# The order of TensorE's instructions in the attention: the scheduler's or the program's

## The chip, the cores and the metric

The kernel runs on one core of a Trainium2 chip. The core has a matrix engine (TensorE, PE in the rows; its weight loads are PEld), a vector engine (VectorE, DVE), an engine for activations (ScalarE, ACT), GpSimd (POOL) and SyncE (SP), which issues most of the loads. Each engine takes its own instructions from a queue of its own, and they wait for each other by semaphores. The metric is the time of one execution on the device in microseconds.

## The reference

One sequence of 512 tokens with 1024 features passes a state-space layer with a gated FFN, then an attention layer with a second gated FFN. The change is in the attention, which has 16 heads of 64 features:

```python
k, v = split(rms_norm(h, kv_norm) @ w_kv);  k = rms_norm(k per head);  q = rms_norm(xn @ w_q per head)
z = (q . k) / 8;  causal = k_pos < q_pos
log_beta = log_sigmoid(z);  log_1m = where(causal, log_beta - z, 0)
later = reverse cumsum of log_1m over the keys - log_1m
w = where(causal, exp(log_beta + later), 0)
out = w @ v;  h = h + out @ w_o
```

## The kernel before

The kernel is written with a layer that records instructions and orders them when the program is built: a scheduler goes through them with estimated durations and sets the order on each engine, by readiness and by their place in the program. A stretch of the program inside `tc.manual_schedule(engines={...})` keeps its written order on the engines named. The state-space layer's part has such a stretch for TensorE; the attention before has none.

The matrices are held as sums of two halves of lower precision (hi and lo), so a product with a weight matrix is three matmuls. Weights arrive by DMA (`t_wraw`); ScalarE makes `t_whi` (L116 or L119) and VectorE `t_wlo` (L130 or L133).

The attention's program is one list of TensorE work woven from two. The main list is the projection of k, q and v for four groups of four heads (L457 to L459, 12 matmuls at a step; `project`), and after it the output projection (L249 to L251, `wo_part`). The side list is the attention of eight pairs of heads. Group 0 is projected first; then `MAIN_RATIO` (0.792) side steps are taken for each main step, and `WO_RATIO` (0.743) in the output projection. A side step ends at each "|" of this list, which is gone through once for each pair p ("-" means pair p - 1, "+" pair p + 1):

```python
PAIR = (
    "|", "z Y0", "z X0", "|", "z X1", "p- A", "t- C0", "z Y1", "t- C1", "p- C", "|", "|", "|", "z Z", "tr+ 0",
    "tr+ 2", "t A0", "|", "tr+ 1", "t B", "|", "|", "p B", "|", "tr+ 3", "|", "t A1",
)
```

- "tr": L516, four transposes that turn the keys or queries of one head (0: keys of head 0, 1: queries of head 0, 2 and 3: of head 1) into PSUM bank 5 or 7. Queries are copied out by ScalarE (L520). Keys are copied out three times, one after the other: L524 (VectorE), L525 (ScalarE), L526 (VectorE).
- "z": L535, the scores of some blocks, into banks 2 to 4. ScalarE takes two sigmoids of them (L557, L558), VectorE a reversed running product by blocks (L564) and the product of both (L565), which is the weight `a_w`.
- "t": L579, four transposes of blocks of `a_w` into bank 5 or 7; ScalarE copies them out to `a_wt` (L581). Transposes of "tr" and "t" take banks 5 and 7 by turns.
- "p": L590, the value products of head 0 and head 1 into the lower and upper 64 partitions of bank 6. "p B" has two of 256 columns, "p A" two of 384 and two of 128, "p C" two of 512. After "p C" the bank is copied out (L608 or L164).

On VectorE and ScalarE there is also the work on the projections: L469 and L464 copy the projection's banks 0 and 1 out, L471 squares them, L474 sums, L475 to L207 are a chain of small operations for the norm, L483 applies it, L489 and L490 split the result into halves. L647 adds the output projection to the stream.

Of the kernel before, what the change touches and what calls it, by code (L numbers as in the profile page):

```python
# [17 lines left out]
DC = D // P  # L18
# [132 lines left out]
def split_x(e, srcs, gain, tag="x"):  # L151

    nc = e.nc
    hi = [e.tile([P, T], F32R, f"{tag}hi{i}") for i in range(len(srcs))]
    lo = [e.tile([P, T], F32R, f"{tag}lo{i}") for i in range(len(srcs))]
    for i, s in enumerate(srcs):
        split_one(e, s, hi[i], lo[i], None if gain is None else gain[:, i : i + 1])
    return hi, lo


def split_one(e, s, hi, lo, gain=None):
    nc = e.nc
    if gain is None:
        nc.scalar.copy(hi, s)  # L164
        nc.vector.tensor_tensor(out=lo, in0=s, in1=hi, op=ALU.subtract)
    else:
        nc.scalar.activation(hi, s, AF.Copy, scale=gain)
        nc.vector.scalar_tensor_tensor(out=lo, in0=s, scalar=gain, in1=hi, op0=ALU.mult, op1=ALU.subtract)  # L168
# [41 lines left out]
def sum_sq(e, pool, srcs, v=True):  # L210

    nc = e.nc
    acc = e.pt(pool, [P, T], F32, "ssacc")
    for i, s in enumerate(srcs):
        t = e.pt(pool, [P, T], F32, "sstmp", 2) if i else acc
        nc.scalar.activation(t, s, AF.Square)
        if i:
            (nc.vector if v else nc.gpsimd).tensor_tensor(out=acc, in0=acc, in1=t, op=ALU.add)
    return acc


def rstd_cols(e, acc, bank=None):

    nc = e.nc
    ps = e.bank(bank)
    for tb in range(4):
        nc.tensor.matmul(ps[:, tb : tb + 1], acc[:, tb * P : (tb + 1) * P], e.ones[:, 0:1], start=True, stop=True)  # L227
    ms = e.tile([P, 4], F32, "rsms")
    nc.vector.tensor_scalar(out=ms, in0=ps[:, 0:4], scalar1=1.0 / D, scalar2=EPS, op0=ALU.mult, op1=ALU.add)
    r = e.tile([P, 4], F32, "rstd4", 2)  # L230
    rsqrt(e, r, ms, [P, 4], "rs")
    return r
# [15 lines left out]
def mm3(nc, ps, whi, wlo, xhi, xlo, start, stop):  # L248
    nc.tensor.matmul(ps, whi, xhi, start=start, stop=False)  # L249
    nc.tensor.matmul(ps, whi, xlo, start=False, stop=False)  # L250
    nc.tensor.matmul(ps, wlo, xhi, start=False, stop=stop)  # L251
# [131 lines left out]
def attn_consts(e, pool):  # L383
    nc = e.nc
    c = {}
    c["identr"] = e.pt(pool, [P, P], F32R, "identr")
    nc.vector.tensor_copy(c["identr"], e.ident)

    c["edge"] = e.pt(pool, [P, T], F32, "edge")
    nc.gpsimd.memset(c["edge"], 0.0)  # L390
    nc.gpsimd.affine_select(
        out=c["edge"], in_=c["edge"], compare_op=ALU.not_equal, fill=1.0, base=T - P - 1, pattern=[[-1, T]],
        channel_multiplier=1)
    return c


MAIN_RATIO = 0.792
WO_RATIO = 0.743
# [9 lines left out]
WO_PARTS = ((0, 4), (4, 6), (6, 8))  # L408
# [231 lines left out]
def wo_part(e, ws, o, pairs, last):  # L640

    nc = e.nc
    hi = {}
    lo = {}

    def add(d, ps):
        nc.vector.tensor_tensor(out=e.hT[d], in0=ps, in1=e.hT[d], op=ALU.add)  # L647

    if not last:
        for i in pairs:  # L650
            if i >= DIRECT:
                hi[i], lo[i] = o[i]
                continue
            hi[i] = e.tile([P, T], F32R, f"xhi{i}")
            lo[i] = e.tile([P, T], F32R, f"xlo{i}")
            split_one(e, o[i], hi[i], lo[i])
        n = DC // len(pairs)
        for c in range(0, DC, n):
            whi, wlo = ws.take()
            for d in range(c, c + n):  # L660
                ps = e.bank(d % 2)
                col = slice((d - c) * P, (d - c + 1) * P)
                for j, i in enumerate(pairs):
                    mm3(nc, ps, whi[:, j, col], wlo[:, j, col], hi[i], lo[i], j == 0, j == len(pairs) - 1)
                    yield
                add(d, ps)
    else:
        w = {}
        for d0, d1 in ((0, LAST_BANKS), (LAST_BANKS, DC)):
            pss = [e.bank(d) for d in range(d0, d1)]  # L670
            for j, i in enumerate(pairs):
                if i not in w:
                    while i >= len(o):
                        yield
                    hi[i], lo[i] = o[i]
                    w[i] = ws.take()
                whi, wlo = w[i]
                for d, ps in zip(range(d0, d1), pss):
                    col = slice(d * P, (d + 1) * P)
                    mm3(nc, ps, whi[:, 0, col], wlo[:, 0, col], hi[i], lo[i], j == 0, j == len(pairs) - 1)  # L680
                    yield
                    if j == len(pairs) - 1:
                        add(d, ps)


def attention(e, ws, grow, r4=None):

    nc = e.nc
    with e.tc.tile_pool(name="attn", bufs=1, reuse_waits="tile") as pool:
        xhi, xlo = split_x(e, e.hT, None)  # L690
        if r4 is None:
            r4 = rstd_cols(e, sum_sq(e, pool, e.hT, False), 7)
        c = attn_consts(e, pool)
        a = Attention(e, pool, ws, c, grow, xhi, xlo, r4)
        for _ in a.project(0):
            pass
        side = a.schedule()
        n = main = 0
        for g in range(1, 4):
            for _ in a.project(g):  # L700
                main += 1
                while n < main * MAIN_RATIO:
                    next(side, None)
                    n += 1
        n = main = 0
        for lo, hi in WO_PARTS:
            last = hi == DC
            while len(a.o) < (lo + 1 if last else hi):
                next(side)
            for _ in wo_part(e, ws, a.o, range(lo, hi), last):  # L710
                main += 1
                while n < main * WO_RATIO:
                    next(side, None)
                    n += 1

G = 64
NP = 32
# [759 lines left out]
def trunk(tc, a, out):  # L1477
    with ExitStack() as ctx:
        e = Env(ctx, tc)
        nc = e.nc  # L1480
        w_up, w_down = a["ffn_w_up"], a["ffn_w_down"]
        v = Vectors(e, a)
        gkv, gb = v.va[:, 0:8], v.va[:, 8:16]
        ws = WStream(
            e,
            win_plan(a["a_w_in"][0]) + glu_plan(a["a_w_glu"][0]) + ffn_plan(w_up[0], w_down[0], False)
            + attn_plan(a["w_kv"], a["b_w_q"][0], gkv, gb) + wo_plan(a["b_w_o"][0]) + ffn_plan(w_up[1], w_down[1], True))
        s5(e, ws, a["a_norm"][0], a["x"][0], a["a_lam_re"][0], a["a_lam_im"][0], a["a_log_dt"][0], a["a_b_re"][0],
           a["a_b_im"][0], a["a_c_re"][0], a["a_c_im"][0], a["a_d"][0], v.load)
        r4 = ffn(e, ws, v.va[:, 16:24], v.cw[0], v.cb[0])  # L1490
        attention(e, ws, v.gr[0], r4)
        ffn(e, ws, v.va[:, 24:32], v.cw[1], v.cb[1], out[0])
# [21 lines left out]
```

## Time and profile before

| | us |
|---|---|
| median of 3 runs | 1261.51 (1259.55 to 1262.16) |
| the profiled execution | 1260.37 |
| its span | 1258.6 |
| TensorE busy | 1218.1 |
| VectorE busy | 780.2 |
| ScalarE busy | 542.2 |

The span is the time from the first to the last instruction of the profiled execution; the execution's own time has 1.8 us around it. An engine's busy time counts each moment once, also where several of its instructions overlap. The attention takes the time from 612 us to about 881 us, where the last value products are, and the end of the output projection after that; a stretch is given in microseconds from the span's start. In the timeline, an instruction's length reaches beyond the start of the next, since matmuls overlap; what an instruction costs the queue is the time from its start to the next one's start. A value product of 32-bit numbers shows as two instructions there.

### The profile page before, as it was taken

To read this page: it belongs to the slowest core of one execution; us is meant where nothing else is said; L and a number is where in the kernel's file an instruction comes from. 1 tells how busy PE (TensorE), PEld (TensorE's weight loads), DVE (VectorE), ACT (ScalarE), POOL (GpSimd) and SP (SyncE) were. 2 spreads that over 40 slices of the span, in tenths; PEclk is the share of its full clock that TensorE was granted. 3 is DMA by queue.
4 is the path that set the end of the run, shared out by engine and by line. 5 is a ranking of instruction groups with operands and counts; after the bars stand their busy time and mean duration, and the time that the engine had idled before them with its cause. 6 is when DMAs were issued, how large, how long until landed. Compare 5 with 4: busy or idle time off the path is not lost. (4 is left out here: it accounts for less than half of the span.)

```text
span 1258.6 us, 17176 instructions
## 1 busy us (share of the span) xinstructions
PE 1218.1 (97%) x6815; PEld 1013.4 (81%) x6815; DVE 780.2 (62%) x1252; ACT 542.2 (43%) x869; POOL 146.3 (12%) x133
## 2 busy tenths in 40 slices
PE   7687899999999999999999999999999999999998
PEld 7677687888888888888999888876788888888887
DVE  9888644867655564333579798875775555562222
ACT  7554543445333333222357675644553343332110
POOL 5869540000000000000000000000300000000000
PEclk9898999999999999999999999999999999999999
DMA  7333232333333333333232111111223333322330
GB/s 204 86 86 89 71 86 89 96 100 99 89 97 101 100 90 92 98 96 95 90 96 68 51 59 56 55 51 51 84 84 101 90 94 101 101 96 88 119 116 34
DMA packets 162379, 111.68 MB, mean 89 GB/s; under 512 B 7452, under 2 KB 151868, under 8 KB 162236
## 3 DMA queue, kind: packets, MB, share of 16 engines
q1 hardware_dynamic: 161724, 109.55, 29.6%
q8 instruction: 53, 0.87, 0.3%
q10 hardware_dynamic: 576, 1.05, 0.2%
q14 instruction: 26, 0.21, 0.1%
HBM read 101.93 MB, written 2.10 MB: 83 GB/s over the span
## 5 line engine op out<-in xcount | busy, mean ns | idle before, releaser
L249 PE MATMUL b<-t_xhi,t_whi 128*128 128x512 f32 x864 | 336.9, 392 | 1.4 <-ACT p_w L1322 1.4
L250 PE MATMUL b<-t_xlo,t_whi 128*128 128x512 f32 x864 | 337.1, 391 | 0.8 <-DVE t_xlo L168 0.7
L251 PE MATMUL b<-t_xhi,t_wlo 128*128 128x512 f32 x864 | 337.3, 391 | 0.2 <-DVE t_wlo L130 0.2
L116 ACT CAST t_whi<-t_wraw 128x1024 fp32r<-128x1024 f32 (+1 forms) x166 | 172.6, 1042 | 364.1 <-PE b L250 243.8
L130 DVE TENSOR_TENSOR t_wlo<-t_wraw,t_whi 128x1024 fp32r<-128x1024 f32 x152 | 184.9, 1218 | 155.3 <-ACT t_whi L116 154.3
L249 PEld LDWEIGHTS b<-t_xhi,t_whi 128*128 128x128 f32 x864 | 162.3, 188 | 37.6 <-issue 2.1
L250 PEld LDWEIGHTS b<-t_xlo,t_whi 128*128 128x128 f32 x864 | 162.4, 188 | 36.5 <-DVE t_xlo L168 2.7
L251 PEld LDWEIGHTS b<-t_xhi,t_wlo 128*128 128x128 f32 x864 | 162.4, 188 | 34.7 <-DVE t_wlo L130 0.6
L457 PE MATMUL b<-t_whi,t_xhi 128*128 128x256 f32 x384 | 109.6, 286 | 0.0
L458 PE MATMUL b<-t_wlo,t_xhi 128*128 128x256 f32 x384 | 109.2, 285 | 0.0
L459 PE MATMUL b<-t_whi,t_xlo 128*128 128x256 f32 x384 | 108.7, 285 | 0.0
L314 DVE TENSOR_TENSOR p_fg<-b,p_rsrow 128x512 f32<-128x512 f32 x44 | 30.4, 691 | 87.0 <-PE b L251 80.6
L457 PEld LDWEIGHTS b<-t_whi,t_xhi 128*128 128x128 f32 x384 | 73.3, 191 | 1.6 <-issue 1.2
L459 PEld LDWEIGHTS b<-t_whi,t_xlo 128*128 128x128 f32 x384 | 73.1, 191 | 1.5 <-issue 1.4
L458 PEld LDWEIGHTS b<-t_wlo,t_xhi 128*128 128x128 f32 x384 | 73.5, 191 | 0.3
L325 DVE TENSOR_TENSOR p_fv<-b,p_rsrow 128x512 f32<-128x512 f32 x44 | 30.4, 690 | 69.6 <-PE b L251 69.6
L249 PE MATMUL b<-p_ahi,t_whi 128*128 128x512 f32 x176 | 69.3, 394 | 0.0
L250 PE MATMUL b<-p_alo,t_whi 128*128 128x512 f32 x176 | 69.3, 394 | 0.0
L251 PE MATMUL b<-p_ahi,t_wlo 128*128 128x512 f32 x176 | 69.3, 394 | 0.0
L348 PE MATMUL b<-t_wlo,p_ahi 128*128 128x512 f32 x176 | 69.3, 394 | 0.0
L347 PE MATMUL b<-t_whi,p_ahi 128*128 128x512 f32 x176 | 69.0, 392 | 0.0
L349 PE MATMUL b<-t_whi,p_alo 128*128 128x512 f32 x176 | 68.3, 388 | 0.0
(305 smaller groups left out, 1917.3 us busy)
## 6 DMA issues: line engine op xcount, KB each, us to landing
t_wraw<-in_ffn_w_up_dram SPq DMA_DIRECT2D x88, 512.0 KB, 3.9
t_wraw<-in_ffn_w_down_dram SPq DMA_DIRECT2D x30, 512.0 KB, 3.4
t_wraw<-in_a_w_glu_dram SPq DMA_DIRECT2D x16, 512.0 KB, 3.6
t_wraw<-in_w_kv_dram SPq DMA_DIRECT2D x16, 512.0 KB, 3.4
t_wraw<-in_ffn_w_down_dram SPq DMA_DIRECT2D x16, 448.0 KB, 3.6
t_wraw<-in_a_w_in_dram SPq DMA_DIRECT2D x8, 512.0 KB, 3.6
p_w<-p_w2d SPq DMA_DIRECT2D x32, 128.0 KB, 2.3
t_wraw<-in_b_w_q_dram SPq DMA_DIRECT2D x8, 512.0 KB, 3.4
```

The source lines that it names most:

```text
L116: nc.scalar.copy(hi, t)
L130: eng.tensor_tensor(out=lo, in0=t, in1=hi, op=ALU.subtract)
L249: nc.tensor.matmul(ps, whi, xhi, start=start, stop=False)
L250: nc.tensor.matmul(ps, whi, xlo, start=False, stop=False)
L251: nc.tensor.matmul(ps, wlo, xhi, start=False, stop=stop)
L314: nc.vector.tensor_tensor(out=g, in0=pg, in1=rr, op=ALU.mult)
L347: nc.tensor.matmul(pss[tb], xh, whi[:, j], start=k + j == 0, stop=False)
L348: nc.tensor.matmul(pss[tb], xh, wlo[:, j], start=False, stop=False)
L349: nc.tensor.matmul(pss[tb], xl, whi[:, j], start=False, stop=st)
L457: nc.tensor.matmul(reg[tb], xh, whi[:, j], start=st, stop=False, skip_group_check=True)
L458: nc.tensor.matmul(reg[tb], xh, wlo[:, j], start=False, stop=False, skip_group_check=True)
L459: nc.tensor.matmul(reg[tb], xl, whi[:, j], start=False, stop=k == 7, skip_group_check=True)
```

## The change

TensorE's instructions in the attention, from the first projection to the end of the output projection, are put in a stretch with the program's order. The instructions are the same; the other engines' orders are still made by the scheduler.

```diff
--- before.py
+++ after.py
@@ -691,27 +691,29 @@
         if r4 is None:
             r4 = rstd_cols(e, sum_sq(e, pool, e.hT, False), 7)
         c = attn_consts(e, pool)
-        a = Attention(e, pool, ws, c, grow, xhi, xlo, r4)
-        for _ in a.project(0):
-            pass
-        side = a.schedule()
-        n = main = 0
-        for g in range(1, 4):
-            for _ in a.project(g):
-                main += 1
-                while n < main * MAIN_RATIO:
-                    next(side, None)
-                    n += 1
-        n = main = 0
-        for lo, hi in WO_PARTS:
-            last = hi == DC
-            while len(a.o) < (lo + 1 if last else hi):
-                next(side)
-            for _ in wo_part(e, ws, a.o, range(lo, hi), last):
-                main += 1
-                while n < main * WO_RATIO:
-                    next(side, None)
-                    n += 1
+        with e.tc.manual_schedule(engines={mybir.EngineType.PE}):
+            a = Attention(e, pool, ws, c, grow, xhi, xlo, r4)
+            for _ in a.project(0):
+                pass
+            side = a.schedule()
+            n = main = 0
+            for g in range(1, 4):
+                for _ in a.project(g):
+                    main += 1
+                    while n < main * MAIN_RATIO:
+                        next(side, None)
+                        n += 1
+            n = main = 0
+            for lo, hi in WO_PARTS:
+                last = hi == DC
+                while len(a.o) < (lo + 1 if last else hi):
+                    next(side)
+                for _ in wo_part(e, ws, a.o, range(lo, hi), last):
+                    main += 1
+                    while n < main * WO_RATIO:
+                        next(side, None)
+                        n += 1
+
 
 G = 64
 NP = 32
```

The value products, TensorE before. The rows are from pair 2 (bank `b_6_6788`); `a_wt` are the transposed weights, `a_v` the values:

```order
L590 MATMUL b_6_6788<-a_wt,a_v 64x256 x2
L579 MATMUL b_5_6868<-t_ident,a_w 128x128 x4
L535 MATMUL b_4_6955<-a_kpad_5266,a_fmq 128x512
L535 MATMUL b_4_6955<-a_kpad_5267,a_fmq 128x512
L590 MATMUL b_6_6788<-a_wt,a_v 64x384
L579 MATMUL b_7_6967<-t_ident,a_w 128x128 x4
```

The first two products of 256 columns stand side by side, a product of 384 columns stands alone. Later in the same pair each of the two products of 512 columns stands alone too; this is the second of them, among the projections:

```order
L458 MATMUL b_0_7073<-t_wlo,t_xhi_5222 128x256
L459 MATMUL b_0_7073<-t_whi,t_xlo_5230 128x256
L457 MATMUL b_0_7073<-t_whi,t_xhi_5222 128x256
L590 MATMUL b_6_6788<-a_wt,a_v 64x512
L516 MATMUL b_5_7058<-p_identr,a_ks 128x128 x4
L458 MATMUL b_0_7073<-t_wlo,t_xhi_5222 128x256
```

TensorE in the changed kernel, the same pair (its bank is now `b_6_6790`), from "z X1" of the pair after it to "p C":

```order
L535 MATMUL b_4_6957<-a_kpad_5268,a_fmq 128x512
L535 MATMUL b_4_6957<-a_kpad_5269,a_fmq 128x512
L590 MATMUL b_6_6790<-a_wt,a_v 64x384 x2
L590 MATMUL b_6_6790<-a_wt,a_v 64x128 x2
L579 MATMUL b_7_6969<-t_ident,a_w 128x128 x4
L535 MATMUL b_2_6976<-a_kpad_5268,a_fmq 128x256
L535 MATMUL b_2_6976<-a_kpad_5269,a_fmq 128x256
L535 MATMUL b_2_6976<-a_kpad_5268,a_fmq 128x384
L535 MATMUL b_2_6976<-a_kpad_5269,a_fmq 128x384
L579 MATMUL b_5_6988<-t_ident,a_w 128x128 x4
L590 MATMUL b_6_6790<-a_wt,a_v 64x512 x2
```

The two products of 384 columns stand side by side, and so do those of 512. Between them are the transposes "t C0" (bank 7) and "t C1" (bank 5) and the scores "z Y1" (`b_2_6976`). On ScalarE, the rows that belong to these read, in the changed kernel:

```order
L557 ACTIVATE a_cp_5280<-b_4_6957 128x512
L558 ACTIVATE a_w<-b_4_6957 128x512
L581 COPY a_wt<-b_7_6969 128x512
L557 ACTIVATE a_cp_5278<-b_2_6976 128x512
L558 ACTIVATE a_w<-b_2_6976 128x512
L581 COPY a_wt<-b_5_6988 128x512
```

Each pair of L557 and L558 are the two sigmoids of one bank of scores; the copy of "t C1" (`b_5_6988`) stands behind those of "z Y1".

The transposes "t A0" of pair 2, TensorE before (`b_5_6719`), where they stand among the projections, some hundred instructions behind the scores they belong to (`b_4_6691`):

```order
L457 MATMUL b_1_6843<-t_whi,t_xhi_5222 128x256
L458 MATMUL b_1_6843<-t_wlo,t_xhi_5222 128x256
L459 MATMUL b_1_6843<-t_whi,t_xlo_5230 128x256
L457 MATMUL b_1_6843<-t_whi,t_xhi_5222 128x256
L579 MATMUL b_5_6719<-t_ident,a_w 128x128 x4
L458 MATMUL b_1_6843<-t_wlo,t_xhi_5222 128x256
L459 MATMUL b_1_6843<-t_whi,t_xlo_5230 128x256
```

The same in the changed kernel (`b_5_6721`, scores "z Z" in `b_4_6693`):

```order
L459 MATMUL b_1_6632<-t_whi,t_xlo_5229 128x256
L535 MATMUL b_4_6693<-a_kpad_5262,a_fmq 128x256
L535 MATMUL b_4_6693<-a_kpad_5263,a_fmq 128x256
L535 MATMUL b_4_6693<-a_kpad_5264,a_fmq 128x256
L535 MATMUL b_4_6693<-a_kpad_5265,a_fmq 128x256
L516 MATMUL b_5_6705<-p_identr,a_ks 128x128 x4
L516 MATMUL b_7_6713<-p_identr,a_ks 128x128 x4
L579 MATMUL b_5_6721<-t_ident,a_w 128x128 x4
L457 MATMUL b_0_6631<-t_whi,t_xhi_5222 128x256
```

The transposes now follow the scores and the two transposes of the next pair's keys at once, and they write bank 5 anew, which "tr+ 0" has written just before, with four transposes between.

VectorE at this place, before: from the copy of the keys out of bank 5 to the last one of the same bank (`b_5_6703`):

```order
L524 CAST a_kpad_5264<-b_5_6703 128x512
L565 TENSOR_TENSOR a_w<-a_w,a_cp_5278 128x256
L524 CAST a_kpad_5266<-b_7_6711 128x512
L565 TENSOR_TENSOR a_w<-a_w,a_cp_5278 128x256
L490 TENSOR_TENSOR a_ks<-a_kh,a_ks 128x16x64
L133 SCALAR_TENSOR_TENSOR t_wlo<-t_wraw,t_va,t_whi 128x256 x3
L526 CAST a_kpad_5265<-b_5_6703 64x512
```

and in the changed kernel (`b_5_6705`):

```order
L524 CAST a_kpad_5266<-b_5_6705 128x512
L524 CAST a_kpad_5268<-b_7_6713 128x512
L133 SCALAR_TENSOR_TENSOR t_wlo<-t_wraw,t_va,t_whi 128x256 x3
L564 SCALAR_TENSOR_TENSOR a_cp_5280<-a_cp_5280,p_edge 128x256 x2
L490 TENSOR_TENSOR a_ks<-a_kh,a_ks 128x16x64
L565 TENSOR_TENSOR a_w<-a_w,a_cp_5280 128x256
L526 CAST a_kpad_5267<-b_5_6705 64x512
```

The scans and products that belong to "z Z" (`a_cp_5280`) now stand between the copies; before, the scans stood ahead of them.

## Rows read from the trace of the kernel before

**Rows 1.** The page: span, and TensorE's busy time, share of the span, instructions.
```profile
span 1258.6 us, 17176 instructions
...
PE 1218.1 (97%) x6815; PEld 1013.4 (81%) x6815; DVE 780.2 (62%) x1252; ACT 542.2 (43%) x869; POOL 146.3 (12%) x133
```

**Rows 2.** Stretch: length, busy PE, PEld, DVE, ACT, POOL (instructions), clock, DMA, GB/s.
```profile
690.00:770.00 80.00, 80.00 (x592) 67.78 (x592) 68.68 (x149) 50.99 (x103) 4.92 (x2) 1.00 0.18 60
```

**Rows 3.** What TensorE waited for, 690 to 930 us: total us, times, longest.
```profile
PE b L250 <- DVE t_xlo L168: 0.7, 2, 0.5
PE b L251 <- DVE t_wlo L130: 0.2, 1, 0.2
```

**Rows 4.** TensorE's timeline from 690 us: start, us, instruction, shape, count.
```profile
690.16 0.65 PE L590 MATMUL b<-a_wt,a_v 128*64 128x256 f32 x4
690.74 0.66 PE L579 MATMUL b<-t_ident,a_w 128*128 128x128 f32 x4
691.33 0.86 PE L590 MATMUL b<-a_wt,a_v 128*64 128x384 f32 x2
692.12 0.39 PE L459 MATMUL b<-t_whi,t_xlo 128*128 128x256 f32 x1
...
695.21 1.07 PE L590 MATMUL b<-a_wt,a_v 128*64 128x512 f32 x2
696.21 0.53 PE L516 MATMUL b<-p_identr,a_ks 128*128 128x128 f32 x4
696.58 0.35 PE L457 MATMUL b<-t_whi,t_xhi 128*128 128x256 f32 x1
```

**Rows 5.** VectorE by shape, 560 to 1010 us: busy us, mean ns, idle before.
```profile
L133 DVE SCALAR_TENSOR_TENSOR t_wlo<-t_wraw,t_va,t_whi 128x256 fp32r<-128x256 f32 x96 | 45.3, 513 | 18.6 <-ACT t_whi L119 18.6
L130 DVE TENSOR_TENSOR t_wlo<-t_wraw,t_whi 128x1024 fp32r<-128x1024 f32 x34 | 42.8, 1260 | 15.5 <-ACT t_whi L116 15.3
...
L524 DVE CAST a_kpad<-b 128x512 fp32r<-128x512 f32 x16 | 11.0, 685 | 2.4 <-PE b L516 2.2
L526 DVE CAST a_kpad<-b 64x512 fp32r<-64x512 f32 x16 | 11.0, 685 | 2.4 <-ACT a_kpad L525 2.0
...
L564 DVE TENSOR_TENSOR_SCAN a_cp<-a_cp,p_edge 128x256 f32<-128x256 f32 x16 | 10.1, 672 | 0.0
L483 DVE TENSOR_TENSOR a_kh<-a_raw,a_hf 128x1024 f32<-128x1024 f32 x8 | 9.8, 1222 | 0.2
L474 DVE TENSOR_REDUCE a_hms<-a_kh 128x16 f32<-128x1024 f32 x8 | 9.8, 1220 | 3.2 <-ACT a_kh L471 3.2
...
L565 DVE TENSOR_TENSOR a_w<-a_w,a_cp 128x256 f32<-128x256 f32 x16 | 6.4, 418 | 0.1
...
L490 DVE TENSOR_TENSOR a_ks<-a_kh,a_ks 128x1024 fp32r<-128x1024 f32 x4 | 4.9, 1220 | 0.7 <-ACT a_ks L489 0.7
```

**Rows 6.** ScalarE by shape, same stretch and columns.
```profile
L557 ACT ACTIVATE a_cp<-b 128x512 f32<-128x512 f32 x40 | 24.6, 615 | 6.2 <-PE b L535 5.9
L558 ACT ACTIVATE a_w<-b 128x512 f32<-128x512 f32 x40 | 24.5, 613 | 1.8 <-PE b L579 1.8
L581 ACT COPY a_wt<-b 128x512 f32<-128x512 f32 x40 | 23.3, 593 | 23.2 <-PE b L579 23.1
```

**Rows 7.** Stretches around TensorE's waits at the kernel's start (columns of rows 2).
```profile
37.00:41.40 4.40, 0.00 (x0) 0.00 (x0) 4.31 (x8) 3.25 (x8) 4.32 (x4) 0.50 0.02 4
41.50:47.10 5.60, 5.60 (x26) 5.60 (x27) 5.60 (x7) 2.96 (x11) 5.04 (x6) 0.50 0.47 143
67.60:69.30 1.70, 0.00 (x0) 0.00 (x0) 1.60 (x4) 1.66 (x5) 1.19 (x1) 1.00 0.10 23
69.30:72.70 3.40, 3.39 (x28) 3.39 (x29) 3.40 (x6) 1.04 (x1) 2.29 (x1) 1.00 0.25 60
117.50:121.30 3.80, 0.00 (x0) 0.00 (x0) 3.80 (x6) 1.19 (x2) 3.64 (x4) 1.00 0.49 127
122.30:125.70 3.40, 3.40 (x29) 2.96 (x28) 0.24 (x2) 1.48 (x4) 3.24 (x4) 0.50 0.05 11
```

## The prediction

> **What bounds the kernel now.** I read the page's list of engines first, then the stretches of the attention, then who makes TensorE wait there, and last the order of the instructions before and after. The page has TensorE busy for 1218.1 of 1258.6 us [rows 1]; in the middle of the attention (690 to 770 us) it is busy without a gap, at clock 1.00, while VectorE is busy 69 of 80 us [rows 2]. In the stretch from 690 to 930 us TensorE waits for another engine 0.9 us in all, and that is for the FFN's inputs, after the attention [rows 3]. So the attention lasts as long as TensorE's instructions take one behind the other. Two things can move its time: cheaper neighbours on TensorE, or a wait where there was none. The change does both.
>
> **What gets cheaper: the value products stand in pairs.** These products (L590) write 64 of the 128 output partitions, head 0 the lower half and head 1 the upper. In the timeline two 256-column products that stand side by side take 0.58 us together (690.16 to 690.74). A lone 384-column one takes 0.79 us (691.33 to 692.12), a lone 512-column one 1.00 us (695.21 to 696.21) [rows 4]. From 384 to 512 is 0.21 us, so a lone 256-column one would be 0.79 - 0.21 = 0.58 us: the second of a pair was free. In the order of before, each of the 8 head pairs has its two 384-column products apart, and its two 512-column products apart; in the new order all of them are neighbours, 24 groups where there were 39. That saves 8 x 0.79 + 8 x 1.00 = 14.3 us.
>
> **What is added: waits at the transposes "t A0".** The program's list puts "z Z", "tr+ 0", "tr+ 2", "t A0" with nothing of the projections between. The scheduler had moved the transposes of "t A0" some hundred instructions back; now TensorE stands at them in that place. They have two inputs that are late. They write bank 5, from which the keys of the next pair ("tr+ 0", 0.4 us before) have still to be copied by L524, L525 and L526; and they read the weights from "z Z", which pass L557, L558 (ScalarE), two scans L564 and a product L565 (VectorE). All matmuls of the stage stand behind them in one queue, the projections too, so whatever they wait is lost in full.
>
> How long: VectorE's new order has these rows between the first L524, which can start only when "tr+ 0" is done, and the last input of "t A0". With the durations of [rows 5], for pair 2: 2 x L524 1.37, 3 x L133 1.54, two scans 1.34, L490 1.22, L565 0.42, L526 0.69 = 6.6 us. For the other pairs the same count gives: pair 0, 5.2 (L474 in the place of L133 and L490); pairs 1 and 3, 5.9 (four L133, no L490); pair 4, 8.5 (three L133, L483, L490, two L526); pair 5, 5.1 (one L130 of 1.26); pair 6, 3.8 (nothing foreign). Sum 41.0 us. TensorE has 0.37 us of work between (four transposes of the second head, 696.21 to 696.58 in [rows 4]), 7 x 0.37 = 2.6; left 38.4 us. Pair 7 has no next keys, only the chain from "z Z": 0.62 + 1.34 + 0.42 = 2.4 us [rows 5, 6].
> Bounds: if only the three copies themselves counted, 0.69 + about 0.59 (L525 is taken as long as the copy L581) + 0.69 = 1.95 us, it is 7 x (1.95 - 0.37) = 11 us. If VectorE comes to the first L524 late by one long instruction (L490, 1.22) each time, it is 38.4 + 8.5 = 47. I take 38.4, since rows that stand behind the first L524 in VectorE's order cannot run ahead of it.
>
> **A second wait, at the 512-column pair.** The program has "t- C0", "z Y1", "t- C1", "p- C" in one go. ScalarE's new order copies C1 out (L581) behind the two sigmoids of Y1: from the end of "z Y1" 0.615 + 0.613 + 0.593 = 1.82 us [rows 6], while TensorE has only C1's four transposes to do, 0.58 us (690.74 to 691.33, [rows 4]). Left 1.24 us, in seven pairs 8.7; the last has no "z" and waits for one copy, 0.6. Together 9.3 us. From below it is 0.6 for each, 5 us, if the sigmoids are not in the way; from above twice my value, 19, if the scans hold up the sigmoids' buffers.
>
> **The clock.** The attention of before runs at clock 1.00 [rows 2], so this price comes from the kernel's start. Behind the wait that ends at 41.4 us, TensorE runs at 0.50, half of 2.4 GHz, until 47.1; behind the wait of 117.5 to 121.3 it has 0.50 from 122.3 to 125.7; behind the 1.7 us wait of 67.6 to 69.3 the clock stays at 1.00 [rows 7]. So the waits at "t A0" of 3.4 to 8.1 us should each be followed by such a stretch, the 1.24 us ones not. A stretch of 3.4 us at half clock does 1.7 us of work: 7 x 1.7 = 11.9 us. Bounds: 0, and 7 x 2.9 = 20 (5.7 us at half, as behind the longest wait).
>
> Here the Trainium skill says more (TensorE: Matmul & The Clock Gate, section "A second HAM failure mode: psum-queue depth-cycling"): short idles between groups of matmuls, if they come often, also let the clock fall back and forth. This kernel's 1.7 us wait shows no such fall. By that rule of the Trainium skill the waits at the 512-column pairs would cost clock as well.
>
> **What moves but costs nothing.** SyncE's and GpSimd's orders are the same, so the loads keep their order. The transposes, score products and projections are the same instructions in number; how they follow each other changes a few hundredths of a us per group, which I leave out. The copies out of banks 0 and 1 before the next projection (L469, L464) and the adds of the output projection (L647) keep about as much TensorE work in front as before; I give them 0, and up to 5 us if they are late.
>
> **The sum.** -14.3 + 38.4 + 2.4 + 9.3 + 11.9 = +47.7 us. The profiled execution took 1260.37 us (span 1258.6 and 1.8 around it); the median of the runs is 1.1 higher. 1260.4 + 47.7 + 1.1 = 1309 us.
>
> **Rivals.**
> 1. Only the pairing counts. If the copies and scans reach "t A0" in time, the sum is -14.3 and the time 1247 us. For it: VectorE is idle one seventh of the stage, and "tr+" and "t A0" use few TensorE cycles, so not much need be hidden. Against it: bank 5 is written twice within half a us with three copies between. It decides if the waits stay under 14.3 / 8 = 1.8 us per pair.
> 2. The waits are there, but only the chains themselves count, because VectorE does the foreign rows at a time when TensorE is not waiting: -14.3 + 11 + 2.4 + 5, no clock lost, +4: 1266 us, up to 1285 with half of the foreign rows. Against it is the order within VectorE's queue.
> 3. Every wait drops the clock, the 1.24 us ones too: 8 x 1.7 = 14 more, 1323 us. Against it the 1.7 us wait of [rows 7].
> 4. The change does nothing that is felt: TensorE's order binds no one, 1261 us. The order shows hundreds of rows moved, so this needs gain and loss to cancel.
>
> **How the numbers follow.** My forecast has 64 in 100, with its own range from 1293 (no clock lost, 5 us instead of 9.3 at the 512-column pairs) to 1326 (VectorE late by 8.5, clock 8 more). Rival 1 has 9, rival 2 has 13, rival 3 has 10, rival 4 has 4. A difference of under 0.2% can't be told from none here. Slower: 64 + 13 + 10 = 87; same 4; faster 9. The range of 8 in 10 leaves out rivals 1 and 4 and the lower part of rival 2, so from 1268; to the top, late VectorE (+8.5), the longer clock stretches (+8), late copies (+5) and a third of what ScalarE's bound leaves (+3) give 1334.
>
> **What would show it.** In the new profile: idle time of TensorE before L579 with VectorE (L526 or L565) as the releaser, about 41 us in eight long waits; idle time before L590 with ScalarE's L581 as the releaser, about 9 us; seven stretches of clock 0.50 between 612 and 930 us; and 512-column products whose pair takes 1.0 us in all where the second wasn't late. It is wrong if TensorE shows no idle time before L579, or if these waits are short because the first L524 ran long before.

## The result: 4.7% slower, and the profile after

The changed kernel takes 1318.5 us (median; 1316.9 to 1323.6) against 1260.5 us of the kernel before in the same session: the ratio is 1.0467, 95% interval [1.0442, 1.0491]. The forecast was 1309 us, in a range from 1268 to 1334. The profiled execution is the longest of the four, 1323.57 us. In the changed file only lines from 694 on have moved, by one or two; the lines of the kernel that are named here stand ahead of that.

The page after, to be held against [rows 1]. The last line is the clock granted to TensorE, in tenths, in 40 slices of the span.

```profile
span 1321.8 us, 17178 instructions
...
PE 1233.5 (93%) x6815; PEld 1031.0 (78%) x6815; DVE 776.4 (59%) x1252; ACT 543.8 (41%) x869; POOL 145.8 (11%) x133
...
PEclk9798999999999999999888899888999999999999
```

The span has grown by 63.2 us, TensorE's busy time by only 15.4: most of the loss is idle time. And the slices in the middle, where the attention is, have a clock below 9 tenths. The stretches show both (columns of [rows 2]: length, busy time of PE, PEld, DVE, ACT, POOL, then the clock):

```profile
690.00:770.00 80.00, 65.31 (x455) 56.41 (x453) 47.28 (x107) 39.42 (x80) 2.40 (x1) 0.87 0.13 41
752.50:758.30 5.80, 0.00 (x0) 0.03 (x1) 5.74 (x11) 3.56 (x7) 0.00 (x0) 0.76 0.30 90
758.30:762.30 4.00, 4.00 (x21) 4.00 (x22) 1.00 (x2) 0.59 (x1) 0.00 (x0) 0.50 0.00 0
```

Where TensorE was busy all 80 us of the first stretch [rows 2], it is now busy 65.3, and VectorE does 47.3 us of work there instead of 68.7: none of the engines is busy all the time. (The attention is stretched, so these 80 us hold less of it than before.) The second row is one wait, with TensorE at nothing and VectorE at work for all of it. The third is what follows: TensorE at work, at half of 2.4 GHz. There are ten such stretches (point 4 further down). One of the two longest, which has the end of one wait in it and a second wait of 1.2 us, reads:

```profile
714.60:724.70 10.10, 7.16 (x34) 6.76 (x35) 3.91 (x7) 3.05 (x5) 0.00 (x0) 0.50 0.17 54
```

What TensorE waited for between 605 and 1000 us (total us, times, longest), where [rows 3] had 0.9 us:

```profile
PE b L579 <- DVE a_kpad L526: 33.8, 7, 5.8
PE b L590 <- ACT a_wt L581: 6.0, 10, 2.1
PE b L516 <- DVE a_qs L490: 4.3, 1, 4.3
PE b L579 <- DVE a_w L565: 4.0, 2, 2.3
PE b L516 <- DVE a_kpad L526: 1.2, 1, 1.2
```

The first and fourth rows are the waits at "t A0": 37.8 us. The second is the wait at the 512-column value products. The third and the fifth, 5.5 us, are waits that the prediction does not have.

One of the waits at "t A0" in both timelines (start, duration, instruction). TensorE:

```profile
751.66 0.80 PE L516 MATMUL b<-p_identr,a_ks 128*128 128x128 f32 x8
758.30 1.09 PE L579 MATMUL b<-t_ident,a_w 128*128 128x128 f32 x4 [5.84 <-DVE a_kpad L526]
```

VectorE in the same time:

```profile
752.34 1.28 DVE L524 CAST a_kpad<-b 128x512 fp32r<-128x512 f32 x2
753.54 1.27 DVE L133 SCALAR_TENSOR_TENSOR t_wlo<-t_wraw,t_va,t_whi 128x256 fp32r<-128x256 f32 x3
754.72 1.26 DVE L564 TENSOR_TENSOR_SCAN a_cp<-a_cp,p_edge 128x256 f32<-128x256 f32 x2
755.91 1.20 DVE L490 TENSOR_TENSOR a_ks<-a_kh,a_ks 128x1024 fp32r<-128x1024 f32 x1
757.02 0.42 DVE L565 TENSOR_TENSOR a_w<-a_w,a_cp 128x256 f32<-128x256 f32 x1
757.47 0.68 DVE L526 CAST a_kpad<-b 64x512 fp32r<-64x512 f32 x1
```

This is the list that the prediction read from VectorE's order for pair 2: two copies, three L133, two scans, L490, one product, one copy. From 752.34 to 758.15 it takes 5.81 us. The prediction counted 6.6 from mean durations; the rows here overlap a little, so that their sum is longer than the stretch. TensorE starts 0.15 us behind its end. L133 and L490, 2.5 us of it, are for later work: "t A0" needs neither.

The value products by width, busy us and mean ns, and idle time before them; the kernel before:

```profile
L590 PE MATMUL b<-a_wt,a_v 128*64 128x512 f32 x32 | 17.2, 618 | 0.0
L590 PE MATMUL b<-a_wt,a_v 128*64 128x384 f32 x32 | 13.7, 510 | 0.0
L590 PE MATMUL b<-a_wt,a_v 128*64 128x128 f32 x32 | 6.5, 285 | 0.0
L590 PE MATMUL b<-a_wt,a_v 128*64 128x256 f32 x32 | 5.2, 405 | 0.0
```

and after the change:

```profile
L590 PE MATMUL b<-a_wt,a_v 128*64 128x512 f32 x32 | 17.8, 676 | 6.1 <-ACT a_wt L581 6.0
L590 PE MATMUL b<-a_wt,a_v 128*64 128x384 f32 x32 | 6.9, 512 | 0.0
L590 PE MATMUL b<-a_wt,a_v 128*64 128x256 f32 x32 | 5.2, 405 | 0.0
L590 PE MATMUL b<-a_wt,a_v 128*64 128x128 f32 x32 | 3.1, 273 | 0.0
```

The 384-column products, now side by side, take half. The 512-column ones do not, though they are neighbours in the order. A timeline says why; first TensorE's rows, then two of ScalarE's:

```profile
815.68 1.07 PE L590 MATMUL b<-a_wt,a_v 128*64 128x512 f32 x2 [1.07 <-ACT a_wt L581]
817.15 1.07 PE L590 MATMUL b<-a_wt,a_v 128*64 128x512 f32 x2 [0.39 <-ACT a_wt L581]
```

```profile
815.01 0.62 ACT L581 COPY a_wt<-b 128x512 f32<-128x512 f32 x1
...
816.44 0.65 ACT L581 COPY a_wt<-b 128x512 f32<-128x512 f32 x1
```

The first head's product starts when its copy is done, and is over (1.07 us) before the second head's copy, which stands behind two sigmoids, is.

### The profile page after: what moved, and what is told of

Same layout as the page of the kernel before. It is cut to its first block, busy times and chain, and to the rows that moved or that the text cites. A ratio compares the mean times of both kernels' runs of the same rounds, so it can differ in the third digit from the quotient of the medians.

```text
span 1321.8 us, 17178 instructions
## 1 busy us (share of the span) xinstructions
PE 1233.5 (93%) x6815; PEld 1031.0 (78%) x6815; DVE 776.4 (59%) x1252; ACT 543.8 (41%) x869; POOL 145.8 (11%) x133
## 5 line engine op out<-in xcount | busy, mean ns | idle before, releaser
L249 PE MATMUL b<-t_xhi,t_whi 128*128 128x512 f32 x864 | 341.0, 395 | 1.5 <-ACT p_w L1324 1.4
L457 PE MATMUL b<-t_whi,t_xhi 128*128 128x256 f32 x384 | 116.2, 303 | 0.0
L458 PE MATMUL b<-t_wlo,t_xhi 128*128 128x256 f32 x384 | 113.0, 294 | 0.0
L459 PE MATMUL b<-t_whi,t_xlo 128*128 128x256 f32 x384 | 113.0, 294 | 0.0
L457 PEld LDWEIGHTS b<-t_whi,t_xhi 128*128 128x128 f32 x384 | 78.3, 204 | 6.7 <-issue 6.4
L314 DVE TENSOR_TENSOR p_fg<-b,p_rsrow 128x512 f32<-128x512 f32 x44 | 30.4, 691 | 86.8 <-PE b L251 82.1
L458 PEld LDWEIGHTS b<-t_wlo,t_xhi 128*128 128x128 f32 x384 | 78.4, 204 | 0.3
L459 PEld LDWEIGHTS b<-t_whi,t_xlo 128*128 128x128 f32 x384 | 78.1, 203 | 0.0
L133 DVE SCALAR_TENSOR_TENSOR t_wlo<-t_wraw,t_va,t_whi 128x256 fp32r<-128x256 f32 x96 | 43.6, 501 | 56.0 <-ACT t_whi L119 45.2
L325 DVE TENSOR_TENSOR p_fv<-b,p_rsrow 128x512 f32<-128x512 f32 x44 | 30.4, 690 | 70.4 <-PE b L251 70.4
```

Source lines behind the costliest of these rows:

```text
L133: nc.vector.scalar_tensor_tensor(out=lo[:, k], in0=t[:, k], scalar=gain[:, k : k + 1], in1=hi[:, k], op0=ALU.mult, op1=ALU.subtract)
L457: nc.tensor.matmul(reg[tb], xh, whi[:, j], start=st, stop=False, skip_group_check=True)
L458: nc.tensor.matmul(reg[tb], xh, wlo[:, j], start=False, stop=False, skip_group_check=True)
L459: nc.tensor.matmul(reg[tb], xl, whi[:, j], start=False, stop=k == 7, skip_group_check=True)
```

## The experiments

The second column is the median of each kernel's runs, and the ratio is to the kernel before, from all runs. The columns behind it are from the profiled executions, in us, from TensorE's first L457 of the attention to its last L242. A step is the time from one instruction's start to the next one's, less the idle time between; "half" is how long the clock record shows 0.50.

| kernel | us | ratio | length | idle | steps L590 | other steps | half |
|---|---|---|---|---|---|---|---|
| before | 1260.5 | | 303.6 | 1.0 | 34.9 | 267.7 | 0 |
| after | 1318.5 | 1.0467 [1.0442, 1.0491] | 366.4 | 50.1 | 30.1 | 286.2 | 64.9 |
| e1_a0 | 1302.4 | 1.0328 [1.0313, 1.0344] | 343.9 | 36.9 | 29.1 | 277.9 | 41.0 |
| e2_c | 1315.1 | 1.0437 [1.0417, 1.0458] | 357.8 | 48.5 | 25.4 | 283.9 | 61.4 |
| e3_both | 1304.7 | 1.0350 [1.0335, 1.0366] | 346.9 | 40.2 | 25.5 | 281.2 | 44.4 |
| e6_fill | 1316.4 | 1.0440 [1.0423, 1.0458] | 359.0 | 27.9 | 30.0 | 274.6 + 26.5 | 27.3 |
| e9_late | 1311.7 | 1.0408 [1.0393, 1.0424] | 353.8 | 40.3 | 30.4 | 283.1 | 51.2 |
| e5_dve | 1389.1 | 1.1029 [1.1012, 1.1045] | 432.8 | 111.6 | 27.8 | 293.4 | 119.5 |
| e8_ahead | 1279.5 | 1.0158 [1.0141, 1.0175] | 322.5 | 23.6 | 26.6 | 272.3 | 17.1 |
| e10_space | 1274.0 | 1.0115 [1.0095, 1.0135] | 317.0 | 19.7 | 25.9 | 271.4 | 13.7 |
| e11_copy | 1274.0 | 1.0113 [1.0096, 1.0131] | 317.1 | 19.3 | 26.1 | 271.7 | 17.1 |
| e12_split | 1283.6 | 1.0195 [1.0180, 1.0211] | 325.2 | 18.2 | 34.2 | 272.8 | 13.7 |
| e13_pair | 1251.9 | 0.9929 [0.9916, 0.9943] | 295.0 | 5.9 | 20.9 | 268.2 | 3.4 |

The main theory: the loss is TensorE standing at steps whose inputs are late, with the clock lost behind it, and the pairs are a real gain. The rival: VectorE is simply short, and a fixed order moves the wait about.

**e1_a0: keys and "z Z" two steps earlier.**

```diff
-"p- C", "|", "|", "|", "z Z", "tr+ 0", "tr+ 2", "t A0", "|", "tr+ 1",
+"p- C", "|", "z Z", "tr+ 0", "tr+ 2", "|", "|", "t A0", "|", "tr+ 1",
```

> Against the changed kernel: the scores "z Z" and the key transposes "tr+ 0", "tr+ 2" stand two side steps earlier and "t A0" stays where it was, so two to four us of projection work lie between them. My theory (the wait at "t A0" is the time that VectorE needs from the first key copy to the last input, less the TensorE work between, and the fall of the clock follows from it): TensorE's idle time before L579 falls from 37.9 us to about 14, the stretches at half clock from 64.9 us in all to under 25, and the time from 1318 to about 1280 (1270 to 1292). Rival (VectorE or ScalarE is short of time in this stage, so the wait only moves to the next transposes or to the scores): idle time of TensorE in the attention stays above 40 us and the time above 1305.

```profile
PE b L579 <- DVE a_kpad L526: 14.8, 6, 5.5
PE b L516 <- DVE a_qs L490: 13.2, 4, 7.1
```

1302.4 us, below the rival's 1305 and well above the theory's 1292. Idle time before L579 fell from 37.9 to 16.5 us, but that before the query transposes grew from 5.5 to 13.2: the list now reaches a group's queries before their norm (L490) is done. The half clock fell to 41.0 us, not to under 25. Both were half right: distance pays for the wait, and the fixed order has a next late input.

**e2_c: "p- C" one step later.**

```diff
-"t- C1", "p- C", "|", "|", "|", "z Z",
+"t- C1", "|", "p- C", "|", "|", "z Z",
```

> Against the changed kernel: the two 512-column products "p- C" come one side step later, so about 1.8 us (0.9 in the output projection) of other matmuls lie between the transposes "t- C1" and them. My theory (the second product waits for ScalarE's copy behind two sigmoids, and the pair then runs one after the other): idle before L590 falls from 6.0 us to under 1, the pairs of 512 take 1.0 us together, about 14 us in all, so from 1318 to about 1304 (1300 to 1309). Rival (the products of 512 columns do not run beside each other at all, only the idle time is lost): 6 us less, 1312.

Idle time before L590 went from 6.0 to 1.1 us and its steps from 30.1 to 25.4: the two terms of the 512-column pair, 9.6 us in sum. The profiled executions differ by 7.4 us and the medians by only 3.3; waits before L579 grew by 2.8. The wait is as described, but the pairs are not all cured: in the timeline four of the eight take 1.1 to 1.3 us together, and in the other four one product still runs behind the other. Products that do run beside each other speak against the rival's mechanism; the time, 1315.1 us, is outside the theory's range and nearer to the rival's 1312.

**e3_both: both edits, and the first pair's keys before its queries.**

```diff
-"t- C1", "p- C", "|", "|", "|", "z Z", "tr+ 0", "tr+ 2", "t A0", "|",
+"t- C1", "|", "p- C", "z Z", "tr+ 0", "tr+ 2", "|", "|", "t A0", "|",
...
-        for a in TURNS:
+        for a in (TURNS[0], TURNS[2], TURNS[1], TURNS[3]):
```

> The edits of the two runs above together, and the first head pair's keys are transposed before its queries, so that the first queries have more time. My theory adds the parts: 24 us of wait at "t A0", about 14 of lost clock, 14 at the products, 4 at the first transposes: 1318 - 56 = 1262 (1252 to 1272), that is within 1% of the kernel before. If what remains of waits is under 5 us it is faster than the kernel before, at about 1250. Rival (VectorE or ScalarE is short of time in this stage): above 1290.

```profile
PE b L516 <- DVE a_qs L490: 19.5, 4, 8.2
```

1304.7 us, the rival's case (above 1290): my 1262 was far off, since I had again counted only the waits that I knew. Waits for L490 before L516 came to 19.5 us, four of them. It was not better than e1_a0.

**e6_fill: useless matmuls in the wait.** Fourteen 128x128 products into bank 6 between "tr+ 2" and "t A0"; nothing reads them.

```diff
-"tr+ 2", "t A0",
+"tr+ 2", "fill 14", "t A0",
...
+        def fill(n):
+            ps = e.bank(6)
+            for _ in range(int(n)):
+                nc.tensor.matmul(ps[:, 0:P], e.ident, e.ident, start=True, stop=True)
```

> Against the changed kernel: 14 useless 128x128 matmuls of 0.21 us each (3.0 us at full clock, into bank 6, which nothing reads then) are added between "tr+ 2" and "t A0" in seven pairs: TensorE works for 3 us of each wait there, everything else is the same. The output is not changed by them. My theory (part of the loss is the clock that falls behind long waits): the wait at "t A0" ends at the same moment, the idle time before L579 falls from 37.9 to about 16 us, the stretches at half clock from 64.9 us to under 25, and the time falls by 10 to 18 us, to 1300 to 1308, although 21 us of work are added. Rival (the clock costs nothing that counts, the wait is all): the same time, 1318 within 4.

1316.4 us, by its median the rival's case. The profiled executions say more: the idle time fell by 22.2 us for 26.5 us of filling, a loss of 4.3; yet the stretch became 7.4 us shorter, since the other steps fell by 11.6 us. The time at half clock went from 64.9 to 27.3 us. So 37.6 us less of half clock were worth about 11.6 us. That the clock costs nothing, as the rival has it, does not fit these 11.6 us. In the profiled executions the gain in time is 6.0 us, in the medians only 2.1; the end of the next section comes back to this.

**e9_late: the list of steps starts three steps later.**

```diff
+        for _ in range(3):
+            yield
         for a in TURNS:
...
-WO_RATIO = 0.743
+WO_RATIO = 0.79
```

> Only edit to the changed kernel: the side list of the attention starts three steps later (and the output projection takes 0.79 instead of 0.743 side steps per step, so that the list still ends with it). Theory (the wait at 't A0' is as long as the rows that VectorE's order has between the first L524 and the last input): with the delay the four L133 rows of the weights' split fall outside that stretch; the rows add up to 4.2, 3.8, 5.5, 3.8, 6.7, 3.8, 3.8 us for the seven pairs instead of 41.0 in all, 31.5, so idle time before L579 falls from 37.9 us to about 28; the queries find L490 done, so the 5.5 us before L516 go too; with a little clock 1318 - 10 - 5 - 2 = 1301 us. Rival (VectorE is the engine that is short, and the wait is its backlog, whatever stands in its order at that place): idle before L579 stays at 35 us or more, time 1312 to 1320.

1311.7 us, by its time at the edge of the rival's case and far from the theory's 1301. The trace is nearer to the theory: no wait before L516 is left, as expected; idle time before L579 fell from 37.9 to 30.8 (28 expected), and the part that L526 ends is 28.1 us in seven waits, where the rows of the expectation less 0.37 us each come to 28.9; the wait before L590 rose from 6.0 to 8.6. The rows in VectorE's order set the wait, as the theory has it, with a part that comes back at another place.

**e5_dve: VectorE in the program's order too.**

```diff
-        with e.tc.manual_schedule(engines={mybir.EngineType.PE}):
+        with e.tc.manual_schedule(engines={mybir.EngineType.PE, mybir.EngineType.DVE}):
```

> Only edit to the changed kernel: VectorE's order in the attention is that of the program as well. The rows of the weights' split (L133) and of the norm (L474 to L490) then stand outside the stretch between 'tr+ 0' and 't A0'; between the first L524 and the last L526 there are only the four copies, 2.75 us, with the scans and products of 'z Z' in front of them. Theory (foreign rows make the wait at 't A0' long): the wait is the two sigmoids, scans, products and copies, about 1.2 + 2.2 + 2.75 - 2 = 4 us for each pair instead of 5.2 to 8.5; idle before L579 28 to 32 us, time 1305 to 1312. Rival (a second engine in a fixed order waits for the first and both lose): VectorE itself stands at rows whose input is late (L474 behind ScalarE, L490 behind GpSimd), idle of TensorE grows to above 60 us, time above 1330.

```profile
PE b L579 <- DVE a_kpad L526: 67.8, 7, 14.9
PE b L458 <- DVE t_wlo L133: 32.7, 6, 8.4
```

1389.1 us, the rival's case: with two engines in a fixed order, the weights' split (L133) now comes late for the projections as well. The waits before L579 did not get shorter either. The foreign rows are gone from between the copies, but they stand ahead of them now, and TensorE waits for them all the same. VectorE in the longest of these waits (691.79 to 706.74 us):

```profile
692.75 1.21 DVE L474 TENSOR_REDUCE a_hms<-a_kh 128x16 f32<-128x1024 f32 x1
...
699.73 1.23 DVE L490 TENSOR_TENSOR a_ks<-a_kh,a_ks 128x1024 fp32r<-128x1024 f32 x1 [1.17 <-ACT a_ks L489]
700.87 1.67 DVE L133 SCALAR_TENSOR_TENSOR t_wlo<-t_wraw,t_va,t_whi 128x256 fp32r<-128x256 f32 x4
...
704.58 0.68 DVE L524 CAST a_kpad<-b 128x512 fp32r<-128x512 f32 x1
```

The norm of a group (L474 to L490), four L133 and the products of "z Z" come first, and the first copy only at 704.58. VectorE also stands at late rows, as the rival said: 46.0 us before L474 for ScalarE's L471 and 26.5 us before L490, there for ScalarE's L489 and not for GpSimd. So this run does not separate a foreign row's cost from that of its place.

**e8_ahead: no step before its inputs.** As e9_late and the first-pair edit of e3_both, with this list:

```diff
-"t- C1", "p- C", "|", "|", "|", "z Z", "tr+ 0", "tr+ 2", "t A0", "|", "tr+ 1", "t B",
+"t- C1", "|", "p- C", "tr+ 0", "tr+ 2", "z Z", "|", "|", "|", "t A0", "tr+ 1", "t B",
```

> Program order of TensorE as in the changed kernel, with the list of steps altered so that no step comes before its inputs: keys of the next pair ('tr+ 0', 'tr+ 2') before 'z Z', both right behind 'p- C'; three steps of projection between them and 't A0'; 'p- C' one step behind 't- C1'; the side list starts three steps later, and the first pair transposes both keys before its queries. TensorE then has 6.9 us of matmuls between 'tr+ 0' and 't A0' in the first four pairs and 3 to 5 us in the last three, against rows of 3.5 to 7.9 us in VectorE's order. Theory (the loss is the waits, and the pairs of value products are worth 10 to 14 us): idle time before L579 under 5 us, before L516 under 4, before L590 under 2, nearly no half clock after 660 us, time 1250 to 1262 us. Rival (a fixed order always meets some late input, the wait only moves): idle in all above 20 us, time above 1280.

1279.5 us, 39 us better than the changed kernel, but a miss for the theory, which had 1250 to 1262: the time is at the edge of the rival's case, and the idle time of 23.6 us, 16.4 of it before L579, is inside it. VectorE has a backlog there: around the longest wait (4.17 us, to 830.9 us) it is at work without a break from 817.4 to 833.0 us. The next kernels give it one more step, with the keys apart.

**e10_space and e11_copy.**

```diff
-"p- C", "tr+ 0", "tr+ 2", "z Z", "|", "|", "|", "t A0", "tr+ 1",
+"p- C", "tr+ 0", "z Z", "|", "tr+ 2", "|", "|", "|", "t A0", "tr+ 1",
...
-nc.vector.tensor_copy(b[HD:], ps[:HD])
+nc.scalar.copy(b[HD:], ps[:HD])
```

The last two lines are e11_copy's alone. In both, the step between "p B" and "tr+ 3" is taken out, so that the list keeps its number of steps.

> Edit to the kernel with the keys ahead (e8_ahead): the two key transposes stand apart, 'tr+ 0' before 'z Z' and 'tr+ 2' one step of projection behind it, and 't A0' one step later, right before 'tr+ 1', so that four steps (8.3, 6.9 or 4.6 us of matmuls) stand between 'tr+ 0' and 't A0'. Theory (what is left of the loss is TensorE coming to 't A0' before VectorE's backlog is done, 16.4 us before L579 there, and distance pays for it): idle before L579 5 to 8 us, in all under 14 us, little half clock; 1279.5 - 10 - 3 = 1266 us, 1260 to 1271. Rival (VectorE is behind by as much as TensorE gains, the wait goes on to 'tr+ 1' or 't B'): idle in all stays above 20 us, 1275 to 1283.

> As e10_space, and the copy of the keys' lower half (L526) is ScalarE's instead of VectorE's: 16 copies of 0.69 us, 11 us off VectorE. Theory (the rows on VectorE between keys and 't A0' set the wait): against e10_space a further 4 to 8 us, 1258 to 1263 us, about the time of the kernel before. Rival (ScalarE now brings the copies of the transposed weights and the sigmoids late): idle before L590 and L579 with ScalarE as releaser above 10 us, time not under that of e10_space.

Waits in the two (e10_space first):

```profile
PE b L579 <- DVE a_kpad L526: 7.6, 4, 2.6
PE b L590 <- ACT a_wt L581: 4.2, 5, 1.4
PE b L516 <- DVE a_kpad L526: 2.8, 3, 1.3
PE b L457 <- ACT a_raw L469: 1.9, 2, 1.2
```

```profile
PE b L579 <- ACT a_wt L581: 6.7, 6, 1.9
PE b L579 <- DVE a_w L565: 4.5, 2, 2.4
PE b L590 <- ACT a_wt L581: 4.2, 5, 1.4
```

Distance bought 5.6 us of median (1274.0), less than expected: the time is just under the rival's range, and the idle time, 19.7 us, just under the rival's 20. New small waits appear (L516, L457). With the copy moved off VectorE the time is the same to 0.1 us, a miss for that theory: L526 ends no wait before L579 any more, and ScalarE's L581 does instead, as the rival had it.

**e12_split: e8_ahead with the pairs taken apart.** The list is shown; `pstep` is cut into the same parts.

```diff
-"p- A", "t- C0", "z Y1", "t- C1", "|", "p- C", "tr+ 0", "tr+ 2", "z Z",
+"p- A0", "t- C0", "p- A1", "z Y1", "t- C1", "|", "p- C0", "tr+ 0", "p- C1", "tr+ 2", "z Z",
```

> Edit to the kernel with the keys ahead (e8_ahead, 1279.5 us, steps of L590 26.6 us): the two 384-column value products stand apart (four transposes between them), the two 512-column ones too, as in the kernel before; nothing else moves. Theory (a second product in the other half of the columns runs beside the first): the steps of L590 grow by 8 us to about 35 us, as in the kernel before; time 1285 to 1290 us. The full price of the pairs, 8 x 0.79 + 8 x 1.00 = 14.3 us, would give 1294. Rival (the neighbours gain nothing that lasts, since TensorE then waits that much longer for VectorE): within 2 us of 1279.5.

The steps of L590 grew by 7.6 us (8 expected), to 34.2, those of the kernel before. The time grew by 4.1 us only, between the theory's range and the rival's: the split products wait nowhere for their copies (4.0 us before L590 in e8_ahead, none here). In the last two head pairs the 512-column products stayed neighbours.

**e13_pair: the scheduler's order, with the pairs.** This edits the kernel before:

```diff
-            nc.scalar.copy(wt[u], ps)
+            last_copy[u] = nc.scalar.copy(wt[u], ps)
...
-            nc.tensor.matmul(
+            mm = nc.tensor.matmul(
...
+            if u in ("A0", "C0") and n >= 384:
+                c1 = last_copy[u[0] + "1"]
+                info = mybir.DependencyInfo(mybir.DependencyClass.Sync, mybir.DependencyReason.DATA)
+                e.tc.add_manual_dep(mm.ins, c1.ins.name, info, reason="pair")
```

> Edit to the kernel BEFORE, not to the changed one: the scheduler orders TensorE as before, but the first of the two 384-column and of the two 512-column value products of a head pair gets a dependency on the second head's copy (L581), so both come ready at the same time; in the new order all 16 stand side by side, as in the changed kernel. Theory (the pairs' gain is real and only the waits of the fixed order cost): no idle time is added, the steps of L590 fall from 34.9 us to about 20.6 us, 1259.6 - 14.3 = 1245 us, 1244 to 1250. If, as with the split (7.6 us), a part of the products still starts with its neighbour late, 1252. Rival (TensorE is not the only bound, and what it saves comes back as waits for VectorE, busy 69 of 80 us): 1257 to 1261 us.

The value products there (L591, one line further down), by width:

```profile
L591 PE MATMUL b<-a_wt,a_v 128*64 128x512 f32 x32 | 8.6, 618 | 0.0
...
L591 PE MATMUL b<-a_wt,a_v 128*64 128x384 f32 x32 | 6.9, 512 | 0.5 <-ACT a_wt L581 0.5
L591 PE MATMUL b<-a_wt,a_v 128*64 128x256 f32 x32 | 5.2, 404 | 0.0
L591 PE MATMUL b<-a_wt,a_v 128*64 128x128 f32 x32 | 3.1, 273 | 0.0
```

and one pair of 512 columns with its neighbour:

```profile
700.72 1.08 PE L591 MATMUL b<-a_wt,a_v 128*64 128x512 f32 x4
701.73 0.54 PE L516 MATMUL b<-p_identr,a_ks 128*128 128x128 f32 x4
```

Both products (x4: each has two records) take the 1.01 us of one. The steps of L590 fell by 14.0 us against 14.3 forecast. 4.9 us of it came back as small waits and about 0.5 in the other steps: 1251.9 us, a ratio of 0.9929 [0.9916, 0.9943]. This is 0.7% faster than the kernel before. That it meets the 1252 of the expectation is luck: that figure was for products that start with their neighbour late, and here they did not; what came back are waits that the theory did not have.

```profile
PE b L579 <- DVE a_kpad L526: 1.8, 2, 1.0
PE b L249 <- DVE t_hT L652: 1.8, 1, 1.8
```

So the rival holds a little too: VectorE's results are now the next to be late.

Taken together: VectorE is not simply short, since the kernel before does the same work on it with 1.0 us of idle time on TensorE, and e13_pair with 5.9. But no list that was tried brought the changed kernel under 18 us of idle time: as the known waits became shorter, others came or stayed. That a list without such waits exists is not shown.

## Why the prediction was right, and where its sizes were not

The direction and the mechanism held; the median came out 9.5 us above the forecast. By the profiled executions the time grew by 63.2 us, the attention by 62.8, against a sum of 47.7.

1. **The pairs, -14.3 us: the size is right, and the order brought a third of it.** e13_pair measured -14.0 when both products are ready together. In the changed kernel the steps of L590 fell by only 4.8 (34.9 to 30.1). The prediction gave the 512-column pair its full gain in one term and the wait in another, as if the second product would still run beside the first.
2. **The waits at "t A0", 40.8 us: 37.9 measured**, eight places, released by L526 and L565: 5.8, 4.8, 5.8, 4.8, 5.5 + 1.7, 4.1, 2.9 and 2.3 us. From pair 1 on it is VectorE's order row for row, and each place is up to 0.9 us under the forecast, since the rows overlap. Pair 0 is 1.0 us above it: VectorE was still at products of earlier scores and came to the first copy only 1.45 us into the wait (and the durations named for pair 0 add up to 5.0, not 5.2). So the sum is closer than its parts. The lower bound of 11, on which rival 2 rested, is out: VectorE did the foreign rows in that place.
3. **The 512-column wait, 9.3 us: 6.0 of idle time, and about 7.5 more that is no idle time**, because the second product runs behind the first (30.1 less the 20.9 of e13_pair is 9.2, less 1.7 for half of its 3.3 us at half clock). That is 13.5 in all, inside the bounds of 5 to 19. This and point 1 are one error: what a late second product costs is the wait and the pair.
4. **The clock, 11.9 us: about 20.** The clock record has ten stretches of 3.4 to 10.2 us, 64.9 in all, where seven were forecast. TensorE worked in 49.2 us of them, so 24.6 is the most they cost; the other steps grew by 18.5 us (267.7 to 286.2), and if all of that is the clock's, with L590's 1.7 it is 20.2, just over the prediction's bound of 20. e6_fill bears it out with 11.6 us for 37.6 us less of it, and in the table the other steps of every kernel with more than 10 us of half clock grow by 0.22 to 0.37 us for each us of it. The step that failed is "a stretch of 3.4 us": the price of one stretch at the kernel's start was taken for all; seven of the ten were twice or three times as long.
5. **What costs nothing, 0 to 5: 5.5 us.** TensorE waited 4.3 us before the first queries and 1.2 us before others. The prediction looked at copies and adds, and not at the query transposes, which stand in the program before the norm of their group is done.

With the measured sizes the sum is -14.0 + 37.9 + 13.5 + 20.2 + 5.5 = 63.1 us, for 62.8 us that the attention grew. It divides the measured length into parts; it is no second test of them.

Rival 1 (only the pairs) is what e13_pair became, by another way than the program's order. Rival 3 (every wait drops the clock) was right that more than seven stretches come: the 2.09 us wait before L590 at 742 us is followed by 3.3 us at clock 0.51, while the 1.07 us wait at 815.7 leaves the clock at 1.00 (rows in the last section). The rule of the Trainium skill (TensorE: Matmul & The Clock Gate, section "A second HAM failure mode: psum-queue depth-cycling"), that frequent short idles between groups of matmuls let the clock go back and forth, agrees with this trace in part, and more than the prediction allowed.

The changed kernel's profiled execution is the longest of its four runs, 5.1 us above their median. The other runs have no trace, but each run's span and mean granted clock are known, and span x 2 x (1 - clock) gives an estimate of its time at half clock, that of the kernel's start included: 95 us in the profiled execution (span 1321.8, clock 0.964), and 82, 71 and 79 us in the others (1317.7, 1315.2 and 1315.6; 0.969, 0.973 and 0.970). The shortest run has 24 us less of it and is 6.6 us shorter, 0.27 us for each, as in the table. So the same kernel loses different amounts of clock in different runs, and in the median run, with about 15 us less of it than in the profiled execution, the clock's term is nearer 16 us than 20 (an estimate). It also tells most of why e6_fill gains 6.0 us in the profiled executions and 2.1 in the medians. By the same estimate e6_fill has 61 us at half clock in its profiled execution and 50, 66 and 58 in its other runs, so that the two kernels lie 35 us apart in the profiled executions and about 21 in the medians. For e2_c (7.4 and 3.3 us) it tells about half; the rest stays open.

## What to carry to other kernels

A written order for one engine is a promise that every input is there when its turn comes; before making it, list for each step what the other engines have in their queues between its inputs' start and their end. A neighbour that is worth having is better asked for by a dependency that makes both instructions ready together than by fixing the whole order: in e13_pair that gave 14.0 us of steps for 4.9 us of waits, where the fixed order gave 4.8 us for 49.1. When a wait is counted, count also what the late instruction would have shared, and the clock behind it.

## What was not expected of the hardware

How long a wait was did not alone tell whether the clock fell. Rows of stretches right behind four waits: in the changed kernel behind 2.09 and 1.07 us,

```profile
742.00:745.30 3.30, 3.30 (x4) 0.56 (x4) 3.30 (x8) 1.40 (x3) 0.00 (x0) 0.51 0.00 0
...
815.70:819.10 3.40, 3.01 (x12) 1.32 (x13) 3.40 (x8) 1.39 (x3) 0.00 (x0) 1.00 0.00 0
```

in e8_ahead behind 2.47 us, and in e9_late behind two waits of 0.87 and 1.33 us whose ends are 2.4 us apart:

```profile
712.40:715.80 3.40, 2.83 (x24) 2.65 (x25) 2.69 (x6) 1.66 (x3) 0.00 (x0) 1.00 0.00 0
```

```profile
705.60:709.00 3.40, 3.40 (x9) 1.79 (x10) 3.30 (x7) 0.00 (x0) 0.00 (x0) 0.51 0.47 154
```

The 2.47 us wait left the clock at 1.00, the two shorter ones did not. In the changed kernel itself all ten waits of over 2 us before one instruction were followed by 0.50.
